# Low parts of the weights in the first half of the tokens: from PoolE to VectorE, with new figures for the planner

## The chip, the cores and the metric

The kernel runs on one core of a Trainium2 chip. Its engines work beside each other, each through its own queue in order: TensorE (PE) multiplies matrices into PSUM, VectorE (DVE) and ScalarE (ACT) work element by element on SBUF and PSUM, PoolE (GpSimd, POOL) does so on SBUF, and SyncE (SP) issues most of the DMA transfers. Semaphores are what makes one queue wait for another. The metric is the device time of one execution in microseconds, lower is better; the output must agree with the reference in float32.

## What is computed

A decoder block on 2048 tokens of width 1024. All that matters here is the first step, one large projection of the tokens to 9216 columns, and that its parts are then used in different ways:

```python
proj = x @ w_in[l] + b_in[l]
q, k, v, g_attn, u_lru, g_lru, gate_logits = jnp.split(proj, SPLIT_POINTS, axis=-1)
q = rope(q.reshape(B, S, N_GROUPS * HEADS_PER_GROUP, HEAD_DIM))
k = rope(k.reshape(B, S, N_GROUPS * HEADS_PER_GROUP, HEAD_DIM))
...
attn = attn.reshape(B, S, ATTN_OUT_WIDTH).astype(dt) * jax.nn.silu(g_attn)
u = causal_depthwise_conv(u_lru, conv_w[l], conv_b[l])
h = rg_lru(u, lru_wr[l], lru_br[l], lru_wi[l], lru_bi[l], lru_lambda[l]).astype(dt)
y_b = (h * jax.nn.silu(g_lru)) @ w_lru_proj[l]
gates = jax.nn.sigmoid(gate_logits).reshape(B, S, N_BRANCHES, D)
merged = gates[:, :, 0] * y_a + gates[:, :, 1] * y_b
out = merged @ w_out[l] + b_out[l]
x = layer_norm(DEEPNORM_ALPHA * x + out, ln_gain[l], ln_bias[l])
```

q and k are 1536 columns each (12 tiles of 128), v as many, the attention's gate 512, the recurrence's input and gate 1024 each, the merge gates 2048: 72 tiles of 128 columns, W below.

## The kernel before

**Precision.** A float32 product is made of three fast matmuls. Each operand is split into a high part (a copy into the narrower type `fp32r`) and a low part (the operand minus its high part): high by high, high by low and low by high are added up in PSUM. The low part of a tile of W, `l`, is one subtraction of 128x512 elements; its high part `h` is a copy on ScalarE.

**Tiling.** The projection, the long first part of the kernel, takes two tiles of W at a time (a pair), 36 pairs for the first 1024 tokens (the first half, `plan[s][0]` is 0) and the same 36 for the other 1024. A pair times two blocks of 512 tokens, with the 1024 rows of W in two halves, is a 2 by 2 by 2 block product. The first two pairs of each half do it plainly, eight products (`plan[s][2]` is None). The other 34 use Strassen's scheme in Winograd's form, seven products; a product is one slot of the plan, 12 matmuls of 128x128 by 128x512 into one PSUM bank of eight (`product`, L623 on). For this they need sums of W's quarters: four quarters A11, A12, A22, A21 come as they are or become the units S1 to S4. In the first half S1 and S3 are begun by an accumulating DMA from PoolE's queue (`added`, L255) and S2 and S4 made by two additions on VectorE (`sums`, L260). In the second half the accumulation is not used, and there are four additions.

**Splitting the units.** `prep_w(s, j)` (L278) splits unit j of pair s: ScalarE copies the high part at once, and a slot later (`later(1, low)`) an engine subtracts for the low part and the raw slot is given back. In the first half of the tokens the units j = 0, 2, 4, 6 have it on PoolE and j = 1, 3, 5 on VectorE; for the plain pairs VectorE does all. Two slots on, SyncE writes the low parts to HBM (`wl_scr`, L310), and in the second half they come back from there by `load_lo` (L312), so that the 34 Winograd pairs there make no low part of W at all. A unit is split five slots before its product.

**The order of the work** is worked out when the program is built. The loop over `where` (L879 on) goes slot by slot. In each it emits a product, then the events that fall due at fixed slots (loads, sums, `prep_w`), then what `later` put off, then side work, then the evacuation of the product's bank. All engines' queues are in this order, and nothing is reordered at run time.

**Side work** is a set of generators (`chains`): the rotation of q and k (`qk_chain`), the transposition of v, the gates, the recurrence (`lru`). A generator yields an `Ask` before each step: how many slots to wait (`lag`), how many free SBUF slots it needs, and what the step costs each engine in microseconds. Every slot adds LEN = 2.75 us of budget to each of the engines' accounts (`left`), fixed work is charged by `spend`, and `run_chains` (L200) lets a step go as long as none of the accounts it draws on is used up; a debt is carried on. The figures in `Ask` and `spend` are thus never a wait on the chip: they set in which slot, and so in which place of the queues, an instruction stands.

**The rotation** in `qk_chain` is: two copies on ScalarE that swap the halves (`sw`, L337, L338); then `rw * cos` on VectorE and `sw * sin` on PoolE (L340 to L345); then the sum of the two on VectorE (L349 or L354), which for the groups of heads with dilation also reorders the tokens; then the store. It runs 48 times in each half, c = 0, 1 being the first half's blocks of tokens and c = 2, 3 the second's; 32 of the 48 have g > 0.

Nearly all additions, subtractions and products go through the helper `tt` and have its line, L240, in the profile, whatever their engine; in a row `l<-S,hS` is the low part of a sum, `l<-wA,hA` and `l<-wS,hS` those of loaded quarters, `sw<-sw,sin` and `y<-y,cos` are parts of the rotation, `y<-y,h` the recurrence's last product. L640 is the matmul of `product`.

After the projection come attention with the recurrence's projection beside it, and the output with the layer norm. The diff doesn't touch them, but they start in SBUF that the projection's slots have left.

Of the kernel before, what the change touches and what calls it, by code (L numbers as in the profile page):

```python
# [11 lines left out]
ALU = mybir.AluOpType  # L12
# [19 lines left out]
def hybrid_block_kernel(ctx: ExitStack, tc: tile.TileContext, a: dict, out: bass.AP):  # L32
    nc = tc.nc
    sp, act, dve, pool, pe = nc.sync, nc.scalar, nc.vector, nc.gpsimd, nc.tensor

    def flat(t):
        return t.bitcast(F32)
# [75 lines left out]
    def later(lag, fn):  # L113
        late.append((now["n"] + lag, fn))
# [37 lines left out]
    def take(name, dt=F32R):  # L152
        if not vacant:
            raise RuntimeError(f"no slot at {now['n']}: {[x[1].name if hasattr(x[1],'name') else x[1] for x in home.values()]} chains {len(chains)}")
        i = vacant.pop(0 if now["n"] < now["last"] else vacant.index(min(vacant, key=LAST_SLOTS.index)))
        t = sl_p.tile([P, CH], dt, tag=f"s{i}", name=name)
        home[id(t)] = (i, t)
        return t

    def give(*ts):  # L160
        for t in ts:
            vacant.append(home.pop(id(t))[0])

    def give_sent(*ts):

        for t in ts:
            later(2, lambda t=t: give(t))
# [3 lines left out]
    def take_lo(name):  # L171

        i = lo_vacant.pop(0)
        return i, sl_p.tile([P, 2, CH], F32R, tag=f"lo{i}", name=name)
# [17 lines left out]
    def spend(**eng):  # L192
        for k, v in eng.items():
            left[k] = left.get(k, 0.0) - v
# [44 lines left out]
    def tt(eng, out, in0, in1, op):  # L239
        eng.tensor_tensor(out=out, in0=in0, in1=in1, op=op)  # L240


    U, LO, raw = {}, {}, {}

    def load_w(s, n, eng=sp):
        r = raw[s, n] = take(f"w{n}_{s}", F32)
        eng.dma_start(r.rearrange("p (k f) -> p k f", f=P), w_part(s, "A21" if n[0] == "S" else n))
# [12 lines left out]
    def sums(s):  # L260
        def add(n, x, y):
            t = raw[s, n] = take(f"{n}_{s}", F32)
            tt(dve, t, raw[s, x], raw[s, y], ALU.add)
        if plan[s][0]:
            add("S1", "S3", "A22")
        add("S2", "S1", "A11")
        add("S4", "S2", "A12")
        if plan[s][0]:
            tt(dve, raw[s, "S3"], raw[s, "S3"], raw[s, "A11"], ALU.add)
            spend(DVE=2.6)  # L270
        else:
            spend(DVE=1.8)

    def by_head(t, mixed=True):

# [2 lines left out]
    def prep_w(s, j):  # L278

        n = units_of(s)[j]  # L280
        r = raw.pop((s, n))
        h = take(f"h{n}_{s}")
        heads = by_head if plan[s][4] == "qk" else (lambda t, mixed=True: t)
        act.activation(heads(h), heads(r, False), AF.Copy)  # L284
        spend(ACT=.66)
        if (s, j // 2) not in LO:
            LO[s, j // 2] = take_lo(f"l{j}_{s}")
        l = LO[s, j // 2][1][:, j % 2]
        if plan[s][2] is None or not plan[s][0]:
            eng = pool if j % 2 == 0 and plan[s][2] else dve  # L290

            def low():
                tt(eng, heads(l), heads(r, False), heads(flat(h)), ALU.subtract)
                if eng is pool:
                    spend(POOL=1.55)
                else:
                    spend(DVE=.93)
                give(r)

            if s:  # L300
                later(1, low)
            else:
                low()
        else:
            give(r)
        U[s, n] = (h, l)
        if plan[s][2] and not plan[s][0] and (j % 2 or j == 6):
            jj = j - j % 2
            t = LO[s, j // 2][1][:, 0:j - jj + 1]
            later(3, lambda: sp.dma_start(wl_scr[plan[s][3]][:, jj:j + 1], flat(t)))  # L310
# [6 lines left out]
    def units_of(s):  # L317
        return ("A11", "A21", "A12", "A22") if plan[s][2] is None else [UNIT[p] for p in plan[s][2]]
# [6 lines left out]
    def blocks(t, g):  # L325

        return t.rearrange("p (r j) -> p j r", r=4 if g == 1 else 16)

    def qk_chain(rw, f, c):
        isq = f < FT_K  # L330
        u = f % 12
        g = u // 4
        nm = f"{f}_{c}"
        yield Ask(lag=2, need=1, ACT=1.3)
        sw = take("sw" + nm)
        scale = 0.125 if isq else 1.0
        act.activation(flat(sw)[lo_], flat(rw)[up_], AF.Copy, scale=scale)  # L337
        act.activation(flat(sw)[up_], flat(rw)[lo_], AF.Copy, scale=scale)  # L338
        yield Ask(lag=1, DVE=1.5 if c < 2 else 1.0, POOL=1.7)
        cos, sin = CS[c % 2]  # L340
        if isq:
            dve.scalar_tensor_tensor(out=flat(rw), in0=flat(rw), scalar=0.125, in1=cos, op0=ALU.mult, op1=ALU.mult)
        else:
            tt(dve, flat(rw), flat(rw), cos, ALU.mult)
        tt(pool, flat(sw), flat(sw), sin, ALU.mult)  # L345
        yield Ask(lag=1, need=1 if g else 0, DVE=(1.45 if c < 2 else 1.2) if g else 1.0)
        if g == 0:
            rp = rw
            tt(dve, flat(rp), flat(rw), flat(sw), ALU.add)  # L349
            give(sw)  # L350
        else:
            rp = take("rp" + nm)
            v, r = "p (j r) -> p j r", 4 if g == 1 else 16
            tt(dve, blocks(flat(rp), g), flat(rw).rearrange(v, r=r), flat(sw).rearrange(v, r=r), ALU.add)  # L354
            give(rw, sw)
        yield Ask()
        dst = qk_scr["q" if isq else "k", u]
        if g == 2 - (not isq):
            r = 16 if isq else 4
            n = CH // r  # L360
            for h in range(2):
                sp.dma_start(dst[64 * h:64 * h + 64].rearrange("d (r i) -> d r i", r=r)[:, :, n * c:n * c + n],
                             flat(rp).rearrange("(d h) (r i) -> h d r i", h=2, r=r)[h])
        else:
            sp.dma_start(dst.rearrange("(h d) s -> d h s", h=2)[:, :, c * CH:(c + 1) * CH], flat(rp))
        give_sent(rp)
# [200 lines left out]
    plan = []  # L567
# [128 lines left out]
    for s in range(1, NQ):  # L696
        t0 = base[s] - (3 if plan[s][0] else 5)
        if plan[s][2] is None:
            for d, n in ((4, "A11"), (4, "A21"), (3, "A12"), (3, "A22")):
                at(t0 - d, lambda s=s, n=n: load_w(s, n))  # L700
            for j in range(4):
                at(t0 + j, lambda s=s, j=j: prep_w(s, j))
            continue
        if plan[s][0]:
            for d, n in ((5, "A11"), (5, "S3"), (4, "A22"), (4, "A12")):
                at(t0 - d, lambda s=s, n=n: load_w(s, n))
        else:
            for d, n in ((6, "S1"), (6, "S3"), (4, "A11"), (3, "A22"), (3, "A12")):
                at(t0 - d, lambda s=s, n=n: load_w(s, n))
            at(t0 - 4, lambda s=s: added(s, "S1", "A22"))  # L710
            at(t0 - 4, lambda s=s: added(s, "S3", "A11"))
        at(t0 - 1, lambda s=s: sums(s))
        for j in range(7):
            if plan[s][0] and j % 2 == 0:
                at(t0 + (3 if s == NQ - 1 and j == 6 else j - 1), lambda s=s, j=j: load_lo(s, j))
            at(t0 + j, lambda s=s, j=j: prep_w(s, j))
# [139 lines left out]
    early = events  # L856
    events = {}
    prep_w(0, 0)
    for kk in K4:
        one_block("B11", kk)  # L860
# [246 lines left out]
    def weights(hp):  # L1107
# [35 lines left out]
        def store():  # L1143
            for h in range(2):
                pool.dma_start(w_scr[hp].rearrange("(y h) (p i) -> h p y i", h=2, i=P)[h],
                             flat(HL[16 * h:16 * h + 16]).rearrange("p x g i -> p (x g) i"))

        return top, sums, lambda: (shares(), store())

    def load_wh(hp, c):  # L1150
# [181 lines left out]
    for hp in range(3):  # L1332
        e = 4 * (3 * hp + 2) + 4
        for i in range(12):
            c, g = i // 3, (0, 2, 1)[i % 3]
# [259 lines left out]
    for t, tt in enumerate(TT):  # L1595
        c, b = divmod(t, 4)
# [67 lines left out]
```

## Time and profile before

| what | value |
|---|---|
| time, median of 3 runs (lowest, highest) | 2090.26 us (2086.84, 2092.15) |
| the profiled execution's own time | 2088.71 us |
| its span, first to last instruction | 2086.9 us |
| mean granted TensorE clock | 0.999 of full speed |
| HBM read and written | 290.33 MB and 151.52 MB |

A row of a group reads: line, engine, operation, tile written <- tiles read, partitions x elements and type of both, count | busy us in total, mean ns of one | idle time of the engine just before them, and what ended most of it. A row of a stretch reads: from:to, its length, then for each engine the busy us and how many instructions, last the granted clock, the share of time the DMA engines were busy, and GB/s. "PEld" is the loading of weights into TensorE, which overlaps its matmuls. A matmul's own duration overlaps its neighbours' (389 ns each where they start every 225 ns), so TensorE's pace is read from counts. The rows of this profile that matter stand in the prediction.

### The profile page before, as it was taken

How to read it: one execution, taken by the hardware profiler on the slowest of the kernel's cores; microseconds unless marked ns; L12 is line 12 of the kernel's file. 1: busy time of each engine (PE TensorE's matmuls, PEld its weight loads, DVE VectorE, ACT ScalarE, POOL GpSimd, SP SyncE). 2: the span in 40 equal slices, each digit the busy share in tenths (PEclk: the TensorE clock that was granted, in tenths of full speed). 3: DMA queues.
4: the chain of work that ended last, by engine and by line, in shares of the span. 5: the costliest groups of instructions: out<-in, count | busy, mean ns of one | idle time of the engine just before them, and what ended most of it. 6: DMA issues, size and time to landing. Idle time of an engine off the chain costs nothing.

```text
span 2086.9 us, 35271 instructions
## 1 busy us (share of the span) xinstructions
PE 2063.8 (99%) x11877; PEld 1687.3 (81%) x11877; DVE 1693.4 (81%) x2990; ACT 1203.2 (58%) x2476; POOL 760.9 (36%) x685
## 2 busy tenths in 40 slices
PE   9999999999999999999999999999999999999998
PEld 7888888888888888888888888787888788788886
DVE  8889999989987757888887888795676676886767
ACT  6475475486466455775776887876666664321100
POOL 2545545645654100120120111114457678521120
PEclk9999999999999999999999999999999999999999
DMA  7868878878887766576576676569878886774431
GB/s 234 240 197 245 247 223 247 261 210 245 251 254 234 267 192 187 184 223 192 187 226 178 200 228 205 164 203 312 212 223 227 239 234 196 238 238 158 142 101 71
DMA packets 335877, 444.20 MB, mean 213 GB/s; under 512 B 167264, under 2 KB 176512, under 8 KB 332624
## 3 DMA queue, kind: packets, MB, share of 16 engines
q1 hardware_dynamic: 319056, 409.50, 63.6%
q0 software_dynamic: 11744, 23.54, 6.0%
q10 hardware_dynamic: 4896, 8.92, 1.2%
q8 instruction: 94, 1.54, 0.3%
q14 instruction: 87, 0.71, 0.1%
HBM read 290.33 MB, written 151.52 MB: 212 GB/s over the span
## 4 chain that ended last, share of the span: by engine, by line
PE 67%; DMA 3%; DVE 2%; POOL 1%; issue 1%; SPq 1%; ACT 1%; DVEq 0%; ACTq 0%; POOLq 0%
PE q L640 40%; PE yb L1234 7%; PE z L1540 3%; PE z L1539 3%; PE z L1541 3%; PE o L1064 3%; PE pt L1031 2%; PE ya L1507 1%; PE ya L1508 1%; PE ya L1506 1%; PE s L1000 1%; PE g L502 1%; DMA V<-v_scr 1%; PE s L994 1%; POOL hx L1210 1%
## 5 line engine op out<-in xcount | busy, mean ns | idle before, releaser
L640 PE MATMUL q<-xT,hS 128*128 128x512 f32 x1632 | 503.1, 389 | 0.0
L640 PE MATMUL q<-xT,l 128*128 128x512 f32 x1088 | 423.6, 389 | 1.1 <-DVE l L240 1.0
L640 PE MATMUL q<-xB,hA 128*128 128x512 f32 x1344 | 415.9, 391 | 0.0
L640 PE MATMUL q<-xB,l 128*128 128x512 f32 x944 | 367.4, 389 | 0.0
L640 PEld LDWEIGHTS q<-xT,hS 128*128 128x128 f32 x1632 | 305.8, 188 | 65.5 <-issue 2.2
L640 PEld LDWEIGHTS q<-xB,hA 128*128 128x128 f32 x1344 | 251.9, 188 | 56.3 <-issue 4.4
L640 PEld LDWEIGHTS q<-xT,l 128*128 128x128 f32 x1088 | 204.2, 188 | 44.9 <-DVE l L240 2.5
L240 POOL TENSOR_TENSOR sw<-sw,sin 128x512 f32<-128x512 f32 x96 | 150.1, 1568 | 176.5 <-ACT sw L338 169.8
L640 PEld LDWEIGHTS q<-xB,l 128*128 128x128 f32 x944 | 177.3, 188 | 37.0
L240 POOL TENSOR_TENSOR y<-y,h 128x512 f32<-128x512 f32 x27 | 35.0, 1297 | 393.5 <-DVE h L539 392.4
L1016 ACT ACTIVATE pb<-pb 128x192 f32<-128x192 f32 (+1 forms) x384 | 160.6, 422 | 26.1 <-DVE pb L1014 26.1
L640 PE MATMUL q<-xT,hA 128*128 128x512 f32 x544 | 168.2, 390 | 1.1 <-ACT hA L284 1.1
L640 PE MATMUL q<-xB,hS 128*128 128x512 f32 x544 | 167.7, 389 | 0.0
L284 ACT ACTIVATE hS<-S 128x512 fp32r<-128x512 f32 x170 | 108.5, 638 | 98.6 <-DVE S L240 84.1
L284 ACT ACTIVATE hA<-wA 128x512 fp32r<-128x512 f32 x220 | 138.1, 636 | 21.1 <-DVE l L240 4.1
L240 POOL TENSOR_TENSOR l<-wA,hA 128x512 fp32r<-128x512 f32 x68 | 108.5, 1596 | 113.7 <-ACT hA L284 92.5
L1234 PE MATMUL yb<-hx,wl 128*128 128x512 f32 x576 | 148.8, 399 | 0.8 <-POOL hx L1210 0.7
L1234 PEld LDWEIGHTS yb<-hx,wl 128*128 128x128 f32 x576 | 104.7, 188 | 28.9 <-issue 5.9
L640 PEld LDWEIGHTS q<-xT,hA 128*128 128x128 f32 x544 | 101.7, 188 | 23.9 <-ACT hA L284 1.6
L640 PEld LDWEIGHTS q<-xB,hS 128*128 128x128 f32 x544 | 102.0, 188 | 21.9 <-issue 0.7
L1510 POOL TENSOR_TENSOR me<-gA,me 128x512 f32<-128x512 f32 x30 | 47.7, 1605 | 157.5 <-DVE gA L1509 110.5
L1539 PE MATMUL z<-wo,ms 128*128 128x512 f32 x256 | 99.6, 389 | 0.0
(208 smaller groups left out, 4303.8 us busy)
## 6 DMA issues: line engine op xcount, KB each, us to landing
wA<-in_w_in_dram SPq DMA_DIRECT2D x220, 256.0 KB
wl_scr<-l SPq DMA_DIRECT2D x102, 512.0 KB
l<-wl_scr SPq DMA_DIRECT2D x102, 512.0 KB
wS<-in_w_in_dram SPq DMA_DIRECT2D x102, 256.0 KB
wS<-in_w_in_dram POOLq DMA_DIRECT2D x68, 256.0 KB, 6.1
wlr<-in_w_f_dram SPq DMA_DIRECT2D x64, 256.0 KB
mg_scr<-y SPq DMA_DIRECT2D x59, 256.0 KB
v_scr<-vs SPq DMA_DIRECT2D x48, 256.0 KB
```

The source lines that it names most:

```text
L240: eng.tensor_tensor(out=out, in0=in0, in1=in1, op=op)
L284: act.activation(heads(h), heads(r, False), AF.Copy)
L502: pe.matmul(g, gw[hs, l], x[hs], start=(n == 0), stop=(n == 2))
L640: pe.matmul(bank, w[:, ks], x[:, kk, xx], start=(first and i == 0), stop=(last and i == 11))
L1016: act.activation(pp, pp, AF.Exp, scale=-1.0, bias=mm, accum_out=ll)
L1031: pe.transpose(pt[e][:, b, 2 * h + x, :], pdata(p, h, c, c + P)[hs], ident[hs, hs])
L1064: pe.matmul(o[hs, 2 * i + b, :], (V[:, kb // 8, kb // 2 % 4, kb % 2] if g == 2 else V[:, kb % 2, kb // 4, kb // 2 % 2])[:, 64 * h:64 * h + ...
L1234: pe.matmul(YB["t"], w[:, a, k], hx(8 * c + k)[:, b], start=(hf == 0 and m == 0), stop=(hf == 1 and m == 11))
L1510: (dve if i in (6, 7) else pool).tensor_tensor(out=ME[c][:, f], in0=ga, in1=ME[c][:, f], op=ALU.add)
L1539: pe.matmul(z, mh[:, k], w[:, 0, hs], start=(k == 0), stop=False)
L1540: pe.matmul(z, mh[:, k], w[:, 1, hs], start=False, stop=False)
L1541: pe.matmul(z, ml[:, k], w[:, 0, hs], start=False, stop=(k == 7))
```

## The change

All seven low parts of a Winograd pair in the first half are made by VectorE. The planner's figures change with it: a low part is charged .62 us of VectorE instead of .93 (and 1.55 of PoolE for those that were its own), the first half's sums 1.25 instead of 1.8, the rotation's first VectorE step 1.0 instead of 1.5 for c < 2, and its second 1.2 instead of 1.45 for c < 2 where g > 0. For c = 2, 3 these two figures are the same as before.

```diff
     U, LO, raw = {}, {}, {}
+    LOW, SUMS = .62, 1.25
...
             tt(dve, raw[s, "S3"], raw[s, "S3"], raw[s, "A11"], ALU.add)
             spend(DVE=2.6)
         else:
-            spend(DVE=1.8)
+            spend(DVE=SUMS)
...
         if plan[s][2] is None or not plan[s][0]:
-            eng = pool if j % 2 == 0 and plan[s][2] else dve
-
             def low():
-                tt(eng, heads(l), heads(r, False), heads(flat(h)), ALU.subtract)
-                if eng is pool:
-                    spend(POOL=1.55)
-                else:
-                    spend(DVE=.93)
+                tt(dve, heads(l), heads(r, False), heads(flat(h)), ALU.subtract)
+                spend(DVE=LOW)
                 give(r)
...
-        yield Ask(lag=1, DVE=1.5 if c < 2 else 1.0, POOL=1.7)
+        yield Ask(lag=1, DVE=1.0, POOL=1.7)
...
-        yield Ask(lag=1, need=1 if g else 0, DVE=(1.45 if c < 2 else 1.2) if g else 1.0)
+        yield Ask(lag=1, need=1 if g else 0, DVE=1.2 if g else 1.0)
```

## The prediction

> **What bounds the kernel now.** I read the page first (part 1, the engines' busy shares), then the table by stretches of time, then what TensorE waited for, and last VectorE's and PoolE's groups of instructions in the first half of the tokens. That half is 254 slots of twelve matmuls (two pairs of eight slots, 34 of seven).
>
> ```profile
> PE 2063.8 (99%) x11877; PEld 1687.3 (81%) x11877; DVE 1693.4 (81%) x2990; ACT 1203.2 (58%) x2476; POOL 760.9 (36%) x685
> ```
>
> TensorE is busy for 2063.8 of 2086.9 us. All that any change outside its matmuls can win is the 23.1 us between the two. The stretches say where these lie, and whether VectorE's load sets TensorE's pace (the columns are PE, weight loads, DVE, ACT, POOL, the granted clock, DMA):
>
> ```profile
> 0.00:150.00 150.00, 146.79 (x638) 120.22 (x639) 122.82 (x191) 86.84 (x146) 56.16 (x58) 1.00 0.77 223
> 150.00:650.00 500.00, 498.88 (x2208) 407.38 (x2207) 469.69 (x541) 295.24 (x476) 274.82 (x205) 1.00 0.83 244
> 650.00:713.00 63.00, 63.00 (x279) 52.16 (x279) 47.89 (x62) 36.83 (x59) 23.89 (x17) 1.00 0.78 248
> 713.00:1405.00 692.00, 690.87 (x3085) 564.91 (x3085) 569.02 (x815) 495.84 (x781) 96.94 (x68) 1.00 0.64 198
> ...
> 200.00:250.00 50.00, 50.00 (x222) 41.42 (x221) 49.61 (x55) 25.04 (x42) 31.34 (x24) 1.00 0.90 259
> 750.00:800.00 50.00, 50.00 (x222) 41.42 (x221) 27.03 (x39) 24.12 (x43) 5.18 (x4) 1.00 0.71 216
> ```
>
> The first three rows hold 638 + 2208 + 279 = 3125 matmuls, which is 9 to warm up, 254 x 12 = 3048 and 66 of the recurrence's gates, with two counted on both sides of a border: the half ends at 713 us. In it TensorE idles 150.00 - 146.79 + 500.00 - 498.88 = 4.3 us. VectorE is busy there for 122.8 + 469.7 + 47.9 = 640 us, and 94% between 150 and 650. Still the last two rows settle the pace: with VectorE at 49.61 of 50 us and with it at 27.03, TensorE runs the same 222 matmuls (50/222 = 0.225 us each) at the same clock of 1.00. VectorE is nearly full, but it isn't what TensorE waits for. The waits say the same (us in total, times, longest):
>
> ```profile
> PE first_bank L851 <- ACT warm L843: 3.2, 1, 3.2
> ...
> PE q L640 <- DVE l L240: 1.0, 1, 1.0
> PEld q L640 <- DVE l L240: 2.5, 4, 1.4
> ```
>
> Of the 4.3 us, 3.2 are the start, which the change doesn't touch. What is left is 1.1 us, 1.0 of it behind one low part that VectorE made late. The timeline (start, duration) shows how it came about:
>
> ```profile
> 521.65 0.68 DVE L240 TENSOR_TENSOR y<-q,v 128x512 f32<-128x512 f32 x1
> 522.25 0.68 DVE L240 TENSOR_TENSOR l<-wS,hS 128x512 fp32r<-128x512 f32 x1
> 522.85 0.68 DVE L534 SCALAR_TENSOR_TENSOR sq<-sq,e 128x512 f32<-128x512 f32 x1
> ...
> 529.33 1.80 DVE L240 TENSOR_TENSOR S<-wS,wA 128x512 f32<-128x512 f32 x1
> 531.16 1.67 DVE L240 TENSOR_TENSOR S<-S,wA 128x512 f32<-128x512 f32 x1
> 532.75 1.76 DVE L240 TENSOR_TENSOR l<-wA,hA 128x512 fp32r<-128x512 f32 x1
> ...
> 528.81 1.76 POOL L240 TENSOR_TENSOR l<-S,hS 128x512 fp32r<-128x512 f32 x1
> 530.53 1.75 POOL L240 TENSOR_TENSOR l<-wA,hA 128x512 fp32r<-128x512 f32 x1
> 532.24 1.73 POOL L240 TENSOR_TENSOR sw<-sw,sin 128x512 f32<-128x512 f32 x1
> ...
> 534.56 0.19 PEld L640 LDWEIGHTS q<-xT,l 128*128 128x128 f32 x1 [1.44 <-DVE l L240]
> ```
>
> At 522 us, with PoolE idle, VectorE starts an operation every 0.60 us, each shown as 0.68. At 529 each of its three operations overlaps one of PoolE's and takes 1.67 to 1.80, so the low part ends some 3.2 us later than it could have, and the matmul behind it waits.
>
> **The change part by part.** *Moved low parts.* PoolE's groups up to 713 us:
>
> ```profile
> L240 POOL TENSOR_TENSOR l<-wA,hA 128x512 fp32r<-128x512 f32 x68 | 108.5, 1596 | 113.7 <-ACT hA L284 92.5 <-PE q L640 10.8 <-DMA wl_scr<-l 5.9
> L240 POOL TENSOR_TENSOR sw<-sw,sin 128x512 f32<-128x512 f32 x48 | 78.7, 1639 | 12.6 <-ACT sw L338 12.6
> L240 POOL TENSOR_TENSOR l<-S,hS 128x512 fp32r<-128x512 f32 x35 | 53.8, 1537 | 98.6 <-ACT hS L284 92.5 <-DVE S L240 2.7 <-PE q L640 1.9
> L240 POOL TENSOR_TENSOR l<-wS,hS 128x512 fp32r<-128x512 f32 x33 | 53.7, 1627 | 6.3 <-ACT hS L284 3.0 <-PE q L640 2.3 <-issue 1.0
> L240 POOL TENSOR_TENSOR y<-y,h 128x512 f32<-128x512 f32 x11 | 14.3, 1296 | 18.5 <-DVE h L539 17.4 <-PE q L640 1.2
> ```
>
> 68 + 35 + 33 = 136 low parts, 216 us of PoolE, go to VectorE; 48 + 11 = 59 operations on tiles stay on PoolE. At VectorE's undisturbed 0.60 us from start to start, VectorE gets 136 x 0.60 = 82 us more work.
>
> *What VectorE gets back.* Its groups up to 713 us, with a group that reads PSUM (the last row) to compare:
>
> ```profile
> L240 DVE TENSOR_TENSOR l<-wA,hA 128x512 fp32r<-128x512 f32 x44 | 45.5, 1034 | 4.4 <-ACT hA L284 4.4
> L240 DVE TENSOR_TENSOR l<-S,hS 128x512 fp32r<-128x512 f32 x33 | 42.4, 1285 | 0.0
> L240 DVE TENSOR_TENSOR l<-wS,hS 128x512 fp32r<-128x512 f32 x35 | 34.0, 970 | 0.0
> L240 DVE TENSOR_TENSOR S<-S,wA 128x512 f32<-128x512 f32 x34 | 38.0, 1117 | 3.2 <-DMA wA<-in_w_in_dram 1.1 <-PE q L640 0.5
> L240 DVE TENSOR_TENSOR S<-wS,wA 128x512 f32<-128x512 f32 x34 | 32.9, 969 | 2.7 <-DMA wA<-in_w_in_dram 2.7
> L240 DVE TENSOR_TENSOR y<-y,cos 128x512 f32<-128x512 f32 x24 | 29.1, 1212 | 0.0
> L342 DVE SCALAR_TENSOR_TENSOR y<-y,cos 128x512 f32<-128x512 f32 x24 | 26.5, 1103 | 0.0
> ...
> L240 DVE TENSOR_TENSOR u<-e,q 128x512 f32<-128x512 f32 x33 | 22.4, 678 | 3.3 <-PE q L640 2.3 <-issue 0.7 <-ACT e L663 0.3
> ```
>
> Operations whose two operands both lie in SBUF mean 0.97 to 1.29 us; the one that reads PSUM stays at 0.68. Against 0.68 the excess is 121.9 - 112 x 0.68 = 45.7 us in the three rows of l, 70.9 - 68 x 0.68 = 24.7 in the two of S, 55.6 - 48 x 0.68 = 23.0 in the two of y<-y,cos: 93 us in seven rows, over 195 operations of PoolE, 0.48 us each. The smaller groups of the recurrence and the rotation show more of the kind, so 0.48 is a floor for the mean. If the moved 136 take their share with them, VectorE gets 136 x 0.48 = 65 us back, and its load goes from 640 to about 640 + 82 - 65 = 657 of 713 us. Bounds: with no relief at all 722, with all of the 93 us gone 629. I take 657, as the rows give it.
>
> The Trainium skill, SBUF — State Buffer, § Who interferes with whom, says that a VectorE instruction with two SBUF inputs and a GpSimd instruction that reads SBUF exclude each other, the later one waiting to the end of the first. It speaks against the change in one respect, that the 136 new operations are themselves of the kind that can be kept waiting; the fence at 529 us agrees with it, and by it the worst for the 59 that stay would be one full wait each, within the bounds above.
>
> *Waits.* A moved low part waits for ACT's copy into h one slot earlier, as PoolE's did. Ready behind it on VectorE stand the evacuations of the product's banks, the next pair's sums and the chains' steps. The rows of l bound it: VectorE idled 4.4 us in 44 cases and 0.0 in the 68 others, at most 0.1 us each, while PoolE's 92.5 us of waiting are those of an engine with nothing else to do. On SyncE every store of low parts now waits for VectorE alone, and it mostly did so before, since the odd one of each two was VectorE's:
>
> ```profile
> SPq L310 <- DVE l L240: 83.2, 39, 6.7
> SPq L247 <- DVE l L240: 40.4, 10, 6.3
> SPq L247 <- POOL l L240: 12.0, 7, 3.0
> ```
>
> The weight loads (L247) wait for the slots that low parts free. With VectorE no fuller those 12.0 us change hands and don't grow much; the cover is the load's lead of three to six slots (8 us and more at 12 x 0.225 = 2.7 us a slot). PoolE's own queue, with the 68 accumulating DMAs, only gets shorter.
>
> *The planner.* Its figures of the first half shift by 136 x 0.62 + 110 x (0.62 - 0.93) = +50.2 us for low parts (110 were VectorE's already, eight of them those of the two plain pairs), 34 x (1.25 - 1.8) = -18.7 for sums, 48 x -0.5 = -24.0 and 32 x -0.25 = -8.0 for the two steps of the rotation: -0.5 us in all, against 254 x 2.75 = 699 us of budget. So side work is handed out at the same rate, somewhat earlier in q/k pairs and later elsewhere. PoolE's budget gains 136 x 1.55 = 211 us and no longer holds a rotation back. The new figures for the rotation, 1.0 and 1.2, are those that the second half has always used, with PoolE at 96.94 us there, and TensorE ran 690.87 of its 692 us. The sums and rotations of the second half aren't edited.
>
> *The sum.* No matmul is added or removed. The late low part at 534 us had its delay from two PoolE low parts and one rotation; I take its 1.0 us as gone. The execution under the profile took 2088.71 us (span 2086.9 and 1.8 around it), 1.6 under the median of 2090.26. So 2088.7 - 1.0 = 2087.7 for it, or **2089.3 us** against the median.
>
> **Rivals.** *VectorE becomes the bound (slower).* If the relief doesn't come, because the 59 operations left on PoolE now always meet an operation of VectorE with two SBUF operands, then between 150 and 650 us the moved low parts (four in each of some 26 pairs, 500/19) add 104 x 0.60 = 62 us to 469.7: 532 us of work in 500, and TensorE ends 32 us later, 2121 us. It decides from a relief under (62 - 30)/104 = 0.31 us per moved low part; my floor is 0.48. A relief a little under that, in the densest stretches alone, would cost a few us up to some 12: 2092 to 2101. For it speaks that TensorE already waited four times for VectorE's low parts (2.5 us); against it the rows above. One chance in ten.
>
> *VectorE was the bound in disguise (faster).* If TensorE's busy time hid a slower pace, a lighter VectorE would speed it up: the first half could give back at most what VectorE gains, 93 - 82 = 11 us, 2079 us. The Trainium skill, Perfetto Trace Analysis, § Identifying the Most-Contended Engine, calls matmul busy time a bad measure of headroom and points to weight-load busy time, here 81%. Against this rival stand the equal 222 matmuls at 49.61 and 27.03 us of VectorE. Another way to the same side is a shift of TensorE's other idle time, the 23.1 - 4.3 = 18.8 us after 713 us, by a better placing of slots at the end of the planned part; it needs a third of all that. Together 4 in 100.
>
> *It does what it says and nothing follows* is the forecast: 86 in 100, with its own range of 2084 to 2095, since the order of side work and the slots that tiles get differ and can move single waits of 1 to 2 us.
>
> **How the numbers follow.** A measurement of this kernel can tell about 0.3%, 6.3 us, from no change. Faster by more, 0.04: it needs more than five times the idle time that the first half has to give. Within 0.3%, 0.86. Slower, 0.10, the first rival. The range goes from 2083 to 2098 us: the forecast's own, and into the first rival's lower part.
>
> **What would show it.** Right: no low part on PoolE; VectorE's l and S rows at 0.7 to 0.85 us up to 713 us; VectorE's busy time of that half between 629 and 722, near 657; TensorE at 222 matmuls per 50 us all through, the second half starting at 713 give or take 2 us, and its wait for l at 534 us gone. Wrong: waits of TensorE for "DVE l" or of its first matmuls for an evacuated bank, repeated in every q/k pair; rows of l staying above 1.0 us; a second half that starts after 716 us; or a time that differs because the attention part starts differently, which would be the slots and not VectorE's load.

## The result and the profile after

| | before | changed |
|---|---|---|
| time, median of 22 runs each | 2091.39 us | 2087.63 us |
| lowest and highest | 2086.84, 2094.72 | 2085.22, 2090.56 |
| profiled execution, time (span) | 2088.71 us (2086.9) | 2085.96 us (2084.2) |

The ratio is 0.9983, 95% interval 0.9977 to 0.9989: 3.8 us by the medians, where 1.0 was forecast, and within the 0.3% that the forecast called no change. In a second comparison (11 runs of the changed kernel, 27 of the one before) it was 0.9982, 0.9973 to 0.9991. The gain is small and real. Of all runs one fell far out: the kernel with the rotation's figures alone once took 3170.36 us at a granted clock of 0.607, and its median below is of its nine others.

The changed kernel's stretches, columns as before (PE, weight loads, DVE, ACT, POOL, clock, DMA):

```profile
150.00:650.00 500.00, 500.00 (x2217) 409.43 (x2216) 444.30 (x647) 300.08 (x482) 114.81 (x98) 1.00 0.82 244
713.00:1405.00 692.00, 690.87 (x3086) 565.00 (x3085) 567.50 (x816) 494.70 (x780) 97.79 (x68) 1.00 0.64 196
...
0.00:711.00 711.00, 707.79 (x3123) 580.24 (x3124) 614.77 (x928) 420.70 (x681) 153.42 (x143) 1.00 0.81 242
```

TensorE has no idle time left between 150 and 650 us. VectorE, with 136 operations more, is busy for 615 us of the half instead of 640, PoolE for 153 instead of 355. The groups of the changed kernel up to 713 us, VectorE's first, PoolE's last:

```profile
L240 DVE TENSOR_TENSOR l<-wA,hA 128x512 fp32r<-128x512 f32 x112 | 80.7, 722 | 4.2 <-ACT hA L285 4.2
L240 DVE TENSOR_TENSOR l<-wS,hS 128x512 fp32r<-128x512 f32 x68 | 52.7, 776 | 0.0
L240 DVE TENSOR_TENSOR l<-S,hS 128x512 fp32r<-128x512 f32 x68 | 48.6, 715 | 0.0
L240 DVE TENSOR_TENSOR S<-wS,wA 128x512 f32<-128x512 f32 x34 | 25.3, 745 | 3.8 <-issue 2.6 <-DMA wA<-in_w_in_dram 1.2
L240 DVE TENSOR_TENSOR S<-S,wA 128x512 f32<-128x512 f32 x34 | 23.5, 692 | 4.3 <-DMA wA<-in_w_in_dram 2.8
L240 DVE TENSOR_TENSOR y<-y,cos 128x512 f32<-128x512 f32 x24 | 21.9, 915 | 0.0
...
L240 POOL TENSOR_TENSOR sw<-sw,sin 128x512 f32<-128x512 f32 x48 | 76.5, 1607 | 38.8 <-ACT sw L334 38.8
```

The same subtraction that meant 0.97 to 1.29 us before means 0.72 to 0.78 now, the sums 0.69 and 0.75 where they were 1.12 and 0.97. So 248 low parts now take 182 us of VectorE, where 112 took 122. Of these rows only the rotation's product, which works beside PoolE's multiply of the same rotation, still stands at 0.92; its sum for the dilated groups, `rp<-y,sw`, means 1.24 where it meant 1.31.

Where the time came from is seen at the first matmul of the second half of the tokens, the 3049th of `product`. The timelines of the kernel before and of the changed one (start, duration):

```profile
713.28 0.61 PE L640 MATMUL q<-xB,hA 128*128 128x512 f32 x2
```

```profile
711.10 0.62 PE L636 MATMUL q<-xB,hA 128*128 128x512 f32 x2
```

The first half ends 2.2 us earlier. The spans differ by 2.7; the other 0.5 us lie after the projection, where the executions differ among themselves (below). The second half of the projection adds nothing: its stretch from 713 to 1405 us has 690.87 us of TensorE in both.

### The profile page after: what moved, and what is told of

It is laid out like the page before. It is cut to its first block, busy times and chain, and to the rows that moved or that the text cites. A ratio compares the mean times of both kernels' runs of the same rounds, so it can differ in the third digit from the quotient of the medians.

```text
span 2084.2 us, 34993 instructions
## 1 busy us (share of the span) xinstructions
PE 2063.8 (99%) x11877; PEld 1688.7 (81%) x11877; DVE 1663.7 (80%) x3126; ACT 1204.0 (58%) x2476; POOL 560.3 (27%) x549
## 4 chain that ended last, share of the span: by engine, by line
PE 93%; DVE 2%; POOL 1%; DMA 1%; ACT 1%; SPq 1%; issue 1%; ACTq 0%; POOLq 0%; DVEq 0%
PE q L636 65%; PE yb L1230 7%; PE o L1060 3%; PE z L1537 3%; PE z L1535 3%; PE z L1536 3%; PE pt L1027 2%; PE s L996 2%; PE ya L1503 1%; PE ya L1504 1%; PE ya L1502 1%; PE g L498 1%; PE s L990 1%; DMA atr<-at_scr 1%; SPq L817 1%
## 5 line engine op out<-in xcount | busy, mean ns | idle before, releaser
L259 POOL DMA_DIRECT2D wS<-in_w_in_dram x68 | 59.2, 911 | 422.4 <-DMA wS<-in_w_in_dram 185.2
L636 PEld LDWEIGHTS q<-xT,hA 128*128 128x128 f32 x544 | 101.6, 188 | 24.5 <-issue 2.2
L333 ACT ACTIVATE sw<-y 64x512 f32<-64x512 f32 x96 | 60.6, 632 | 70.9 <-DVE y L577 45.5
```

What stands on the lines that cost most here:

```text
L259: pool.dma_start(t, w_part(s, x), accum_op=ALU.add)
L636: pe.matmul(bank, w[:, ks], x[:, kk, xx], start=(first and i == 0), stop=(last and i == 11))
```

## The experiments

What was to be told apart: whether the move of the low parts or the planner's figures brought the gain, whether it came by way of collisions with PoolE or by that of VectorE's load as such, and whether the difference beyond 2.2 us is real. From here on "the half ends" means the start of the second half's first matmul.

**The move alone.** The planner is charged as before, so ScalarE's, SyncE's and TensorE's queues hold exactly the order of before.

```diff
-                tt(eng, heads(l), heads(r, False), heads(flat(h)), ALU.subtract)
+                tt(dve, heads(l), heads(r, False), heads(flat(h)), ALU.subtract)
                 if eng is pool:
                     spend(POOL=1.55)
```

> The low parts move to VectorE and the planner is charged as before (1.55 us of PoolE, .93 of VectorE), so every queue but VectorE's and PoolE's holds the very same order as before. Theory (the collisions between PoolE's low parts and VectorE's operations made four low parts late, 2.2 us in all; the planner's figures do nothing): VectorE's busy time up to 713 us falls from 640 to 610-625 us, no wait of the weight loads for l is left, the second half starts at 711.1 us (before 713.3), ratio 0.998 to 0.9995. Rival (the new figures, that is the new order of side work, brought the gain): the second half starts at 713 us or later and the ratio is 1.000 or above.

Measured: 2087.75 us (9 runs), ratio 0.998, 0.997 to 0.999. The half ends at 710.5 us. Its stretch up to there:

```profile
0.00:711.00 711.00, 707.78 (x3126) 580.22 (x3127) 622.82 (x929) 421.36 (x682) 149.38 (x143) 1.00 0.82 241
```

VectorE at 623 us, and no weight load waits for l. The move alone has the whole gain; the figures and the order that they bring add nothing that can be measured (2087.75 and 2087.63 us).

**The figures alone.** Low parts as before, .93 to .62, 1.8 to 1.25, 1.5 to 1.0, 1.45 to 1.2.

```diff
-                    spend(DVE=.93)
+                    spend(DVE=.62)
...
-            spend(DVE=1.8)
+            spend(DVE=1.25)
...
-        yield Ask(lag=1, DVE=1.5 if c < 2 else 1.0, POOL=1.7)
+        yield Ask(lag=1, DVE=1.0, POOL=1.7)
...
-        yield Ask(lag=1, need=1 if g else 0, DVE=(1.45 if c < 2 else 1.2) if g else 1.0)
+        yield Ask(lag=1, need=1 if g else 0, DVE=1.2 if g else 1.0)
```

> Only the planner's figures change (.62, 1.25, 1.0, 1.2); PoolE keeps its four low parts of seven, at 1.55. Theory: the collisions stay, VectorE's busy time up to 713 us stays at 630 to 650 us, the weight loads still wait for l in a few places, the second half starts between 713 and 716 us, ratio 0.9995 to 1.0015. Rival (the figures brought the gain): the second half starts at 711 to 712 us, ratio 0.998 to 0.999.

Measured: 2112.40 us (5 runs), ratio 1.0095, 1.0079 to 1.0110. Both expectations were wrong in size: the half ends at 735.4 us, 22 us later than before. What the weight loads waited for (us, times, longest):

```profile
PEld q L640 <- DVE l L240: 18.0, 8, 5.0
...
PEld g L502 <- DVE vl L240: 2.4, 3, 1.2
```

The worst place, from the timeline, VectorE's rows and the weight load that waited:

```profile
253.84 2.47 DVE L478 SCALAR_TENSOR_TENSOR v<-ub,lrn,v 128x512 f32<-128x512 f32 x3 [0.82 <-ACT v L476]
256.22 0.68 DVE L240 TENSOR_TENSOR y<-q,u 128x512 f32<-128x512 f32 x1
259.40 3.21 DVE L478 SCALAR_TENSOR_TENSOR v<-ub,lrn,v 128x512 f32<-128x512 f32 x3 [2.49 <-ACT v L476]
262.53 1.76 DVE L240 TENSOR_TENSOR S<-wS,wA 128x512 f32<-128x512 f32 x1
264.38 0.69 DVE L240 TENSOR_TENSOR S<-S,wA 128x512 f32<-128x512 f32 x1
264.99 0.68 DVE L240 TENSOR_TENSOR l<-wA,hA 128x512 fp32r<-128x512 f32 x1
...
265.73 0.29 PEld L640 LDWEIGHTS q<-xT,l 128*128 128x128 f32 x1 [5.01 <-DVE l L240]
```

Here VectorE isn't even full. Two steps of the recurrence were let into its queue ahead of the sums and the low part; VectorE waits 2.49 us for ScalarE inside them, then a PoolE low part stretches the first sum to 1.76, and TensorE stands for 5 us behind all of it. With low parts left on PoolE these figures charge VectorE 18.7 + 32.0 for sums and rotation and 110 x 0.31 = 34.1 us for low parts less than before, 85 us in all, and the planner may let side work go earlier; more of it there is not, VectorE runs 792 operations up to the half's end as before. In the change itself the same figures charge seven low parts a pair instead of three, and the total stays.

**Half of the figures each.** First the rotation's two lines alone, then low parts and sums alone, both on the kernel before.

> The kernel before with the shorter figures of the rotation alone (1.0 and 1.2 for c < 2); low parts stay with PoolE, .93 and 1.8 as before. With all shorter figures the first half grew by 22 us, most of it in two slots of q/k pairs. Theory (the long figures of the rotation held the room that the collisions needed): most of the 22 us come, second half at 725 to 737 us, ratio 1.005 to 1.011. Rival (it is the low parts' and sums' figures): 713 to 716 us, ratio 0.999 to 1.002.

> The kernel before with the shorter figures of low parts and sums alone (.62 and 1.25); the rotation keeps 1.5 and 1.45. Theory (the room lay in the rotation's figures): 713 to 718 us, ratio 0.999 to 1.002. Rival: 725 to 737 us, ratio 1.005 to 1.011. If both halves of the figures cost much less than 22 us, it is the sum of the room that counts, and not whose it was.

Measured: 2095.40 us, ratio 1.0023 (1.0010 to 1.0036), the half ending at 719.9 us, for the rotation; 2093.25 us, 1.0003 (0.9992 to 1.0015), at 715.1 us, for the other. Against 713.3 that is 6.6 and 1.8 us, and 22 together. The rotation's figures held more of the room, but neither theory covers it: together the figures cost far more than the sum of the two.

Part of that is TensorE's clock. In the run with all figures the granted clock stood at 0.50 twice for 6.8 us, from 264.5 and from 431.8 us, each time within and behind a wait of about 5 us. In these two rows of that run it is the third number from the end, and the matmuls at 0.50 start every 0.43 us instead of 0.225:

```profile
250.00:300.00 50.00, 45.41 (x192) 35.96 (x191) 43.01 (x56) 35.01 (x56) 19.39 (x16) 0.93 0.81 229
400.00:450.00 50.00, 44.25 (x186) 34.72 (x185) 42.26 (x50) 25.33 (x44) 18.10 (x16) 0.93 0.72 204
```

TensorE worked 10.5 us at that clock, so by an estimate 5.3 of the 22 us are the clock's. With the rotation's figures it is 1.6 of 6.6 us (0.50 for 3.4 us), with the other figures none. That leaves 17 us against 5 and 1.8, still more than the sum; why, is open. Not every wait has such a stretch behind it: in the rotation's run one of over 3 us, at 259 us, has none.

**The collisions back.** The changed kernel, and PoolE does a subtraction like the former one behind each moved low part. It writes a raw slot that is about to be given back; nobody reads it.

```diff
                 spend(DVE=LOW)
+                if j % 2 == 0 and plan[s][2]:
+                    tt(pool, r, r, flat(h), ALU.subtract)
                 give(r)
```

> The changed kernel, and behind each of the 136 moved low parts PoolE does one more subtraction of the same size in the raw slot that is about to be given back (its result is not used). This is the first rival of the prediction made real: the moved work without the relief. Theory: collisions come back at 0.5 to 0.8 us for each, VectorE's busy time up to 713 us goes from 616 to 684-715 us, TensorE waits for l and for evacuations in the q/k pairs, and the second half starts 3 to 30 us later than 711, ratio to before 1.000 to 1.015. Rival (VectorE has its relief from elsewhere, such as the planner's order): VectorE at 616 to 640 us, second half at 711 to 712 us, ratio 0.998.

Measured: 2114.22 us (4 runs), ratio 1.0107, 1.0093 to 1.0120; the half ends at 735.6 us. Its stretch and its waits:

```profile
0.00:735.00 735.00, 714.68 (x3121) 581.45 (x3122) 696.89 (x928) 420.90 (x680) 380.53 (x279) 0.99 0.80 232
...
PEld q L638 <- DVE l L240: 20.8, 11, 3.5
```

VectorE goes from 615 to 697 us without an instruction more, 0.60 us for each of PoolE's 136: the collisions are the cost. Here is the prediction's first rival, moved work with little relief, and it takes 24.5 us at the half's end where 32 were worked out. Some 4.9 of the 24.5 us, by the same estimate, are the clock's, which was 0.50 three times for 3.4 us. The run isn't quite pure: PoolE's subtraction waits for VectorE's, and the slot is given back later.

**More work for VectorE, no collisions.** One more subtraction on VectorE itself behind each moved low part; and the same behind half of them (`j % 4 == 0`).

```diff
                 spend(DVE=LOW)
+                for _ in range(1 if j % 2 == 0 and plan[s][2] else 0):
+                    tt(dve, r, r, flat(h), ALU.subtract)
                 give(r)
```

> The changed kernel, and behind each of the 136 moved low parts VectorE itself does one more subtraction of the same size in the raw slot (its result is not used): 136 x 0.60 = 82 us more, PoolE as in the changed kernel. Theory (load alone matters little until VectorE is full): VectorE's busy time up to 713 us goes from 616 to about 698 us, between 150 and 650 us to 444 + 62 = 506 of 500, so that it just becomes the bound there: the second half starts 2 to 15 us later than 711, ratio to before 0.999 to 1.007. Rival (VectorE paces TensorE at any load): each us of it costs, the second half starts 60 us later or more, ratio 1.025 and above. Second rival (the banks and the lead of five slots hide it all): 711 us, ratio 0.998.

> The changed kernel with one more subtraction on VectorE behind 68 of the 136 moved low parts (units 0 and 4; its result is not used): 68 x 0.60 = 41 us more, 615 + 41 = 656 us of 711, about the load that the prediction expected for the change itself. Twice as much cost 30 us. Theory (VectorE's load alone costs little until some stretch is full; collisions and bunching are what costs): 711 to 716 us for the start of the second half, ratio to before 0.998 to 1.001. Rival (cost follows the added work in proportion, 30/82 of it): 726 us, ratio 1.005.

Measured: 2120.02 us, ratio 1.0134 (1.0120 to 1.0148), the half ending at 741.5 us, for 136 more; 2087.23 us, 0.9987 (0.9977 to 0.9997), at 710.5 us, for 68 more. The stretches, of 136 first:

```profile
150.00:650.00 500.00, 481.55 (x2091) 385.63 (x2090) 488.32 (x702) 277.25 (x445) 114.70 (x96) 1.00 0.77 225
```

```profile
0.00:711.00 711.00, 707.78 (x3126) 579.95 (x3127) 661.31 (x997) 422.12 (x683) 153.90 (x143) 1.00 0.82 243
...
150.00:650.00 500.00, 500.00 (x2217) 409.35 (x2216) 480.61 (x701) 301.29 (x482) 116.12 (x98) 1.00 0.83 243
```

68 more cost nothing: VectorE at 661 us of 711, and at 481 of 500 where it is fullest, leaves TensorE without a gap. 136 more cost 30 us, twice the upper end of what was expected; VectorE is the bound there, at 488 of 500 and with 25 waits for l; of the 30 us some 1.7 are the clock's (0.50 for 3.4 us). The kernel before had VectorE at 640 and was late at four places. So its load as such didn't make it late.

**Both kernels again.** Unchanged, one execution each under the profile, later the changed one again with runs of its own.

> The kernel before, unchanged, once more under the profile. The first profile of it was of an execution 2.7 us under the median of its runs. Theory (the late low parts of the first half come from chance meetings of PoolE and VectorE): the waits of the weight loads for l come again at about the same places and cost 2 to 5 us, the second half starting at 713 to 716 us; the time after that start is 1373 to 1377 us as in the other profiles. Rival (the gain lies after the projection): the second half starts at 713 us at most and the time after it is 1375 us or more.

> The changed kernel once more under the profile. Theory: no wait of the weight loads for l, the second half starts at 710.5 to 711.5 us in every execution; what differs from one execution to the next (2085 to 2091 us) lies after the projection, in waits for transfers in the attention part. Rival: the start of the second half moves too.

> The changed kernel again, beside the two others on the same chip: second half at 710 to 711.5 us, 712.6 us from there to the last matmul of the projection, ratio to before 0.998 to 0.999.

Measured: the kernel before, in an execution of 2095.79 us, ends its half at 715.5 us, with these waits:

```profile
PEld q L640 <- DVE l L240: 5.2, 7, 1.9
```

The changed kernel ends it at 710.2 and 710.9 us, after 711.1 in the first profile, each time without a wait for l. So the first profile of the kernel before, at 2088.71 us an execution under the median of 2091.39, showed fewer late low parts than the second, an execution 4 us over the median. The mean of the two against the mean of the changed kernel's three is 3.6 us at the half's end, near the 3.8 of the medians. The expectation of 710.5 to 711.5 us in every execution of the changed kernel was a little narrow.

From the half's end to the end of the span the kernel before took 1373.7 and 1378.5 us, the changed one 1373.1, 1377.0 and 1376.6. The expectation for the kernel before, up to 1377, was short, and the cause expected, waits in the attention part, is not what the kernel before shows: TensorE idles 17.7 us after the projection in its first profile and 17.8 in its second. What differs is the granted clock. In the second it was 0.50 for 6.8 us from 1432.2 and for 3.4 us from 1558.5; in the first it was 1.00 up to 2080 us. In the changed kernel's three both differ: idle time of 16.0, 17.9 and 18.5 us, and 3.4, 6.8 and 3.4 us at 0.50 just behind the projection. Why the clock falls there in some executions is open.

**One more wait taken out.** In all profiles TensorE waits at one place of the second half for a high part that ScalarE copies too late. In the changed kernel:

```profile
1338.56 0.80 ACT L517 ACTIVATE tr<-tr,sp 128x512 f32<-128x512 f32 x1
1339.26 0.61 ACT L285 ACTIVATE hA<-wA 128x512 fp32r<-128x512 f32 x1
...
1339.92 0.30 PEld L636 LDWEIGHTS q<-xT,hA 128*128 128x128 f32 x2 [1.55 <-ACT hA L285]
```

```diff
-    t0 = base[s] - (3 if plan[s][0] else 5)
+    t0 = base[s] - ((4 if s == 67 else 3) if plan[s][0] else 5)
```

> The changed kernel, with the weights of one pair of the second half (number 67) split one slot earlier. In every profile so far TensorE waits 1.3 us at one place there, for the high part of that pair's fifth unit, which ScalarE copies behind six activations of the recurrence. If that wait is only a matter of place, it goes: from the start of the second half to the last matmul of the projection 711.1 to 711.3 us instead of 712.6, and the time falls by 1.4 us against the changed kernel, ratio to before 0.9975 to 0.998. If ScalarE or the slots are late elsewhere then, the wait moves to another slot and nothing is gained.

Measured: 2085.66 us (11 runs), ratio to before 0.9977, 0.9966 to 0.9987, beside 2087.33 us and 0.9982 of the changed kernel in the same comparison. TensorE's stretch is whole:

```profile
713.00:1405.00 692.00, 692.00 (x3092) 565.98 (x3091) 569.51 (x818) 496.12 (x782) 97.33 (x68) 1.00 0.64 196
```

The 1.3 us are gone by the profile. By the times the step lies within the intervals, so it is likely, not shown, that this is the fastest of the three.

## Why the prediction was right, point by point

- **TensorE bounds the projection, and only its few waits could be won.** Right. In the changed kernel and in the one with 68 operations more, VectorE's load differs by 46.5 us, and TensorE's first half by 0.6 us.
- **The term of 1.0 us** for the late low part had the right mechanism and too small a size. The half ended 2.2 us earlier against the first profile, 4.4 to 5.3 against the second, 3.6 by the means. Two things were off. I took TensorE's idle time, 1.0 us, where the row quoted beside it, the waits of the weight loads, had 2.5 us in four places: matmul records of 0.39 us started every 0.225 cover the first 0.16 us of each gap. And one profile, from an execution 2.7 us under the later median, was taken as typical. By the starts of the matmuls, slot by slot, the late low parts of the first profile cost 0.3 + 0.4 + 1.3 us.
- **VectorE's load, 657 us,** was too high by 42: it is 615. The relief per moved low part was not 0.48 but (640 + 82 - 615)/136 = 0.79 us, or 0.73 with the move alone and its 623 us. The 0.48 was named a floor, with 629 as the bound below; the measured load lies under that, since the groups of the recurrence and of the rotation, left out of the seven rows, got their share back too (`v<-ub,lrn,v`, for one, went from 31.8 to 24.8 us).
- **The planner's total hardly shifts (-0.5 us), so side work keeps its rate.** Right: with the low parts on VectorE the times agree under the new figures and the old ones, 2087.63 and 2087.75 us. That it was needed to work out the total is shown by the figures alone, where it shifts by -85 and costs 22 us.
- **A moved low part's new wait, at most 0.1 us each:** right, 4.2 us in all, where it was 4.4.
- **The rival "VectorE becomes the bound"** didn't come. Its price, 32 us, lies near the 24.5 of the run with PoolE busy again, but in part by luck: by the prediction's own rule that run has 444 + 62 = 506 us of work for 500, not 532, which would cost 6 us; the rest came from late low parts and 4.9 us of the lower clock. That the cost follows from filling 500 us was too simple at the edge: at 481 of 500 there was none, at 488 there was 30 us over the whole half.
- **The rival "VectorE was the bound in disguise"** fell by the 68 operations more, which cost nothing. The weight loads' busy share, 81%, is the same in the changed kernel, as is TensorE's pace.
- **Not foreseen:** how much the old, longer figures carried. The load of VectorE, the planner's charge against before, the time at half the clock up to the half's end, and that end, over the kernels (us):

| kernel | charge | VectorE busy to the half's end | waits of weight loads for l | granted clock at 0.50 for | half ends |
|---|---|---|---|---|---|
| before, two profiles | 0 | 640, 642 us | 2.5, 5.2 us | 0, 0 us | 713.3, 715.5 us |
| move alone | 0 | 623 | none | 0 | 710.5 |
| changed | -0.5 | 615 | none | 0 | 711.1 |
| changed, 68 more | -0.5 | 661 | none | 0 | 710.5 |
| changed, PoolE busy again | -0.5 | 697 | 20.8 | 10.2 | 735.6 |
| changed, 136 more | -0.5 | 708 | 26.7 | 3.4 | 741.5 |
| before, rotation's figures | -32 | 641 | 7.7 | 3.4 | 719.9 |
| before, low and sum figures | -53 | 651 | 3.8 | 0 | 715.1 |
| before, all figures | -85 | 653 | 18.0 | 13.7 | 735.4 |

Neither the charge nor the load alone orders the ends. With VectorE at 641 us the half ends at 713 or at 720, and with 661 at 710.5. What the late rows seem to have in common, and this is argued and not shown, is that low parts come late where more stands in VectorE's queue ahead of them than the plan counted, by collisions that no figure holds or by figures that are too short. Why 68 plain operations more are free while the 25 us by which VectorE's load in the kernel before exceeds the changed one's are not, is left open: the operations are spread evenly over all pairs and the collisions are not, but no run separates the two.

## What to carry to other kernels

Where one engine is full by the profile, look at how long its instructions take beside the same instruction undisturbed before moving work off it: here an operation brought back from PoolE to the fuller VectorE made VectorE lighter, by 0.73 to 0.79 us of relief against 0.60 of work. A planner's costs that hold room for such collisions are to be changed together with what causes them; here the shorter figures alone cost 21 us, some 5 of them by the clock that fell behind the longest waits, and together with the move they cost nothing, but gained nothing either. And with a bound engine at 99%, read its waits where they are not hidden by pipelined records, in the weight loads or in starts, and from more than one execution.

## What the runs showed of the hardware that I had not expected

A PoolE subtraction of 128x512 in float32 beside a busy VectorE costs VectorE 0.60 us when put back and frees 0.73 to 0.79 when taken away, as much as or more than the 0.60 us that VectorE needs to do it itself; so in these stretches it bought nothing to use PoolE for it. The PoolE operations that stayed hardly got faster without the others: the rotation's multiply means 1607 ns, where it meant 1639. The granted clock of a single core fell to 0.50 for 3.4 or 6.8 us in some of these executions: within and behind waits of 2.2 to 5 us in the first half, in four of the kernels, and just behind the projection in all profiles of the changed kernel.
